# Three one-column tiles of a row norm put into one tile, and the weight tiles behind them 128 bytes lower

## The chip, the cores and the metric

The kernel runs on one core of a Trainium2 chip. A core has a matrix engine (TensorE, PE in the profile), a vector engine (VectorE, DVE), a scalar engine (ScalarE, ACT), GpSimd (POOL), a queue engine that issues most transfers here (SyncE, SP), and 16 DMA engines. Each engine runs its own instructions in order; they wait for each other by semaphores. SBUF is the on-chip memory of 128 partitions; a tile takes the same range of bytes in each partition. PSUM holds the results of matmuls. The metric is the time of one execution of the kernel on the device in microseconds (us), as the median of several runs. Lower is better.

## The reference

One layer of a bidirectional encoder on a sequence of 2048 rows of 1024 float32 values:

```
u      = rms_norm(x) * norm_mix_g
P      = u @ w_in                              # 1024 x 3600
v,x1,x2 = conv3(P[:, :1536])                   # hyena group, 512 channels each
z      = x1 * (h1 * v + d1 v);  z = x2 * (h2 * z + d2 z)     # long convolutions by FFT
q,k    = silu(conv3(P[:, 1536:2560]))          # mLSTM group, 4 heads, two directions
y      = concat(group_norm(z), group_norm(sigmoid(o) * mlstm(q, k, v, gates)))
h      = x + y @ w_out
h      = h + cross_attention(rms_norm(h), rms_norm(mem))     # mem: 256 rows
h      = h + square(relu(rms_norm(h) @ ff_w1)) @ ff_w2
out    = rms_norm(h)
```

rms_norm divides each row by the root of the mean of its squares plus 1e-6 and multiplies by a gain. The change touches the norm of x ahead of w_in and the norm of mem, both computed by the same function.

## The kernel before

**Products.** Every large product in float32 is made of three matmuls in a reduced-precision form: each operand is split into a high part (a cast, ScalarE) and a low part (operand minus the high part, VectorE); `mm3` adds high x high, high x low and low x high. In the profile these are lines L295, L296 and L297; the cast is L300 and the subtraction L301 in `split`. A matmul holds one operand of 128 columns still and streams the other past it, with up to 512 columns.

**Stages.** In the order of the program: the input projection (`sweep` for the columns that are convolved, with streamed blocks of 512 columns of `xh` and `xl`; `natural` for the others, with streamed weight blocks of 256 or 272 columns) is woven with first the filters' generation (`filters`) and then the long convolutions (`hyena`); then the mem projections (`memproj`) woven with the mLSTM; then the output projection and cross-attention (`attention`), then the MLP (`ffn`). By the trace, the first ends at about 1150 us, the mLSTM's weave with the mem projections at about 1400, attention at about 2090 and the MLP at the end.

**Input projection.** One pool of SBUF tiles, `i_sb` (`self.isb`), belongs to it and lives on through the mem projections. x is too large to be kept in split form, so `xh` and `xl` hold 1024 rows of it, transposed, and it is loaded and normalised three times by halves: first half, second half, first half again. With the two blocks of mem that gives 26 calls of `prep_norm` for 128 rows each. Each norm is followed by `prep_turn`: eight transposes on TensorE (L420), a cast (L300) and a subtraction (L301) for each half. `pop` lets one norm after the other go in between the matmul groups of `sweep` and `natural`. The weights come by `weights`: a load into `wn` (L327, from SP), a cast to `wh` (L300), a subtraction to `wl` (L301).

**A row norm.** `prep_norm` lets ScalarE sum the squares of the two halves of a row (L409), adds the sums on VectorE into the one-column tile `ms` (L411), scales and adds epsilon (L412), and calls `rsqrt`, which finds the inverse root on VectorE without a table: a shift and a subtraction on the bits (L150, L151) and three steps of three operations each (L153 to L155) on `y` and `t`, one-column tiles as well. Then `xn` is scaled in place by `y` and the gain (L414). The tiles `ms`, `y` and `t` have two buffers each, and each buffer of a tile of one column of 4 bytes takes 32 bytes of a partition.

**What sets the order.** The kernel is written as generators that `weave` lets run in turn by given weights. A scheduler takes the whole program, estimates times, and orders the instructions of each engine; an instruction that needs a buffer of a tile comes after the last use of the tile that had the buffer before. The order on every queue, SP's too, is fixed at that point. Addresses are given by the order in which a pool's tags are first used: after `ms` come the tags of `rsqrt`, and then `wh`, `wl`, `wn` and `sg`. `xh`, `xl`, `xn`, `st`, `P` and `cv` lie ahead of them.

**Other lines that the steps touch.** In `hyena`: L669 and L670 (loads of `dm` and `em`), L672, L675 and L676 (loads of `a`), L702 and L734 (matmuls in full float32, two passes), L703 and L736 to L740 (the complex product), L705 (store of `zg`), L766, L768 and L769 (norm of the result, its gain, its store `yh`). In the mem projections: `mt`, `kt` (split and transposed mem and keys). In attention: L1028 (load of w_out), L1100 (loads of the rows), L1106 (transposes of them), `act` (their split form).

Of the kernel before, what the change touches and what calls it, by code (L numbers as in the profile page):

```python
# [9 lines left out]
F32 = mybir.dt.float32  # L10
# [87 lines left out]
class Prog:  # L98
# [42 lines left out]
        else:  # L141
            self.nc.vector.tensor_copy(out, in_)

    def rsqrt(self, pool, ms, name):
        nc = self.nc
        shp = list(ms.shape)
        y = pool.tile(shp, F32, tag=name + "_y", name=name + "_y", bufs=2)
        t = pool.tile(shp, F32, tag=name + "_t", name=name + "_t", bufs=2)
        yi, mi = y.bitcast(I32), ms.bitcast(I32)
        nc.vector.tensor_scalar(yi, mi, 1, None, ALU.logical_shift_right)  # L150
        nc.vector.tensor_scalar(yi, yi, -1.0, float(0x5F3759DF), ALU.mult, ALU.add)  # L151
        for _ in range(3):
            nc.vector.tensor_tensor(t, y, y, ALU.mult)  # L153
            nc.vector.scalar_tensor_tensor(t, t, -0.5, ms, ALU.mult, ALU.mult)
            nc.vector.scalar_tensor_tensor(y, t, 1.5, y, ALU.add, ALU.mult)  # L155
        return y
# [247 lines left out]
    def prep_norm(self, xn, gain):  # L404
        nc, sb = self.nc, self.isb
        ss = sb.tile([128, 2], F32, tag="ss", name="ss", bufs=2)
        for h in range(2):
            junk = sb.tile([128, 512], F32, tag="st", name="junk", bufs=3)
            nc.scalar.activation(junk, xn[:, 512 * h:512 * h + 512], AF.Square, accum_out=ss[:, h:h + 1])  # L409
        ms = sb.tile([128, 1], F32, tag="ms", name="ms", bufs=2)  # L410
        nc.vector.tensor_tensor(ms, ss[:, 0:1], ss[:, 1:2], ALU.add)  # L411
        nc.vector.tensor_scalar(ms, ms, 1.0 / D, EPS, ALU.mult, ALU.add)  # L412
        rv = self.rsqrt(sb, ms, "xr")
        nc.vector.scalar_tensor_tensor(xn, xn, rv, gain, ALU.mult, ALU.mult)  # L414

    def prep_turn(self, xn, t):
# [1285 lines left out]
```

## Time and profile before

| | |
|---|---|
| median of 3 runs | 3382.24 us (3379.86 to 3386.33) |
| profiled execution | 3383.48 us |
| span of its trace | 3381.8 us |
| granted TensorE clock, mean | 0.979 |
| TensorE busy | 3194.3 us, 94% |
| weight loads | 2550.0 us, 75% |
| VectorE busy | 2042.5 us, 60% |
| ScalarE busy | 1492.4 us, 44% |
| GpSimd busy | 1269.8 us, 38% |
| HBM | 452.23 MB read, 219.18 MB written |

The span runs from the first to the last instruction of the trace; the time of the execution holds a little more on both sides. The page groups instructions by line, engine, operation and tiles (written as output<-inputs): busy time and the mean duration of one in ns, then the engine's idle time just before them, with what ended it. A matmul's duration there overlaps the next one's, so the rate is read from the distance of the starts. The timeline lists instructions by start (us from the span's start), duration, engine, line and tiles, with "xN" where N like instructions in a row are put together, and in brackets the idle time before them with what released them. The windows view gives each engine's busy time in stretches, the granted clock and the DMA engines' share.

### The profile page before, as it was taken

What the parts mean: (1) busy time and instruction counts of PE and PEld (TensorE: products, weight loads), DVE (VectorE), ACT (ScalarE), POOL (GpSimd) and SP (SyncE); (2) the same over time, 40 slices, a digit from 0 to 9 for tenths busy, and PEclk for the clock granted to TensorE, in tenths of its full rate; (3) what the DMA queues carried; (4) which work ended last, traced back from release to release, by engine and by line L of the source; (5) the groups of instructions that cost most, each with busy time, mean ns of one, the idle gap of its engine ahead of it and who ended that gap; (6) DMA issues with size and microseconds to landing.
All of it is one profiled execution on the core that took longest, in us unless ns stands there. A gap on an engine that the chain in (4) does not pass through costs nothing.

```text
span 3381.8 us, 46860 instructions
## 1 busy us (share of the span) xinstructions
PE 3194.3 (94%) x15671; PEld 2550.0 (75%) x15671; DVE 2042.5 (60%) x3711; ACT 1492.4 (44%) x2884; POOL 1269.8 (38%) x894
## 2 busy tenths in 40 slices
PE   6999999999898888799999999999999999999997
PEld 5646666677676788688887997788788887888876
DVE  7685225524546755777766554755855576555695
ACT  4344435523454235444444444555655543333335
POOL 2131001200222314544424012876766564434482
PEclk9999999999999999999999999999999999999998
DMA  5366889996998579857657444765654475444434
GB/s 165 117 208 206 286 282 256 271 325 238 241 240 279 172 229 273 275 154 231 184 162 253 147 132 161 224 205 179 207 167 158 147 244 171 128 140 135 133 94 159
DMA packets 480749, 674.55 MB, mean 199 GB/s; under 512 B 41738, under 2 KB 256848, under 8 KB 479484
## 3 DMA queue, kind: packets, MB, share of 16 engines
q1 hardware_dynamic: 478904, 668.70, 63.4%
q0 software_dynamic: 1600, 2.86, 0.4%
q8 instruction: 124, 2.03, 0.3%
q14 instruction: 117, 0.96, 0.1%
q10 hardware_dynamic: 4, 0.00, 0.0%
HBM read 452.23 MB, written 219.18 MB: 199 GB/s over the span
## 4 chain that ended last, share of the span: by engine, by line
PE 43%; DVE 7%; DMA 5%; issue 3%; POOL 2%; ACT 1%; SPq 1%; DVEq 0%; ACTq 0%; POOLq 0%
PE mm L295 9%; PE mm L297 9%; PE mm L296 9%; PE hy L297 5%; PE hy L295 4%; PE hy L296 4%; DVE wl L301 1%; DVE bl L1292 1%; POOL acc L1500 1%; DMA rw<-rows 1%; PE hy L1106 1%; DMA wr<-xs 1%; DMA wn<-in_x_dram 1%; DMA va<-vd 1%; DVE acc L1542 0%
## 5 line engine op out<-in xcount | busy, mean ns | idle before, releaser
L301 DVE TENSOR_TENSOR wl<-wn,wh 128x512 fp32r<-128x512 f32 (+1 forms) x352 | 274.6, 813 | 144.4 <-ACT wh L300 143.8
L1292 DVE TENSOR_TENSOR bl<-wr,bh 128x512 fp32r<-128x512 f32 x213 | 234.8, 1108 | 134.6 <-ACT bh L1291 132.2
L1291 ACT CAST ah<-w 128x512 fp32r<-128x512 f32 x284 | 176.2, 622 | 298.9 <-PE hy L296 152.7
L300 ACT CAST wh<-wn 128x512 fp32r<-128x512 f32 (+1 forms) x352 | 202.1, 617 | 216.2 <-PE mm L296 80.0
L295 PE MATMUL mm<-xh,wh 128*128 128x512 f32 x640 | 276.4, 432 | 8.7 <-ACT P L542 7.5
L739 POOL TENSOR_TENSOR b<-b,a 128x512 f32<-128x512 f32 x64 | 88.8, 1387 | 502.1 <-ACT b L737 201.1
L296 PE MATMUL mm<-xl,wh 128*128 128x512 f32 x640 | 266.4, 416 | 0.1
L297 PE MATMUL mm<-xh,wl 128*128 128x512 f32 x640 | 264.3, 413 | 0.3 <-DVE wl L301 0.3
L1292 DVE TENSOR_TENSOR al<-w,ah 128x512 fp32r<-128x512 f32 x236 | 226.9, 963 | 59.9 <-ACT ah L1291 59.7
L1291 ACT CAST bh<-wr 128x512 fp32r<-128x512 f32 x232 | 143.4, 621 | 244.3 <-PE mm L297 180.1
L297 PE MATMUL mm<-bh,al 128*128 128x512 f32 x576 | 224.4, 392 | 8.3 <-DVE al L1292 5.7
L295 PE MATMUL mm<-bh,ah 128*128 128x512 f32 x576 | 226.0, 392 | 0.0
L296 PE MATMUL mm<-bl,ah 128*128 128x512 f32 x576 | 225.0, 391 | 0.0
L295 PE MATMUL mm<-act,wh 128*128 128x512 f32 x512 | 201.4, 397 | 6.0 <-ACT wh L300 6.0
L296 PE MATMUL mm<-act,wh 128*128 128x512 f32 x512 | 203.0, 397 | 0.0
L297 PE MATMUL mm<-act,wl 128*128 128x512 f32 x512 | 201.1, 396 | 0.0
L1149 POOL TENSOR_TENSOR ssum<-ssum,sq 128x512 f32<-128x512 f32 x56 | 80.7, 1440 | 269.7 <-ACT sq L1148 268.2
L295 PE MATMUL hy<-bh,ah 128*128 128x512 f32 x448 | 175.2, 391 | 0.0
L296 PE MATMUL hy<-bl,ah 128*128 128x512 f32 x448 | 174.6, 390 | 0.0
L297 PE MATMUL hy<-bh,al 128*128 128x512 f32 x448 | 174.6, 390 | 0.0
L295 PEld LDWEIGHTS mm<-xh,wh 128*128 128x128 f32 x640 | 122.4, 191 | 56.7 <-issue 18.0
L295 PE MATMUL hy<-xh,ah 128*128 128x512 f32 x384 | 152.8, 398 | 7.6 <-ACT ah L1291 6.8
(379 smaller groups left out, 9021.1 us busy)
## 6 DMA issues: line engine op xcount, KB each, us to landing
wr<-hc SPq DMA_DIRECT2D x224, 256.0 KB
w<-in_ff_w_dram SPq DMA_DIRECT2D x176, 256.0 KB
a<-hd SPq DMA_DIRECT2D x128, 256.0 KB
hc<-t SPq DMA_DIRECT2D x128, 256.0 KB
wn<-in_w_in_dram SPq DMA_DIRECT2D x104, 256.0 KB
hc<-q SPq DMA_DIRECT2D x96, 256.0 KB
fs<-a SPq DMA_DIRECT2D x32, 512.0 KB
a<-fs SPq DMA_DIRECT2D x32, 512.0 KB
```

What stands on the lines that cost most here:

```text
L295: mm(ps, lh, rh, start=start, stop=False)
L296: mm(ps, lh, rl, start=False, stop=False)
L297: mm(ps, ll, rh, start=False, stop=stop)
L300: self.nc.scalar.copy(hi, src)
L301: self.nc.vector.tensor_tensor(lo, src, hi.bitcast(F32), ALU.subtract)
L739: nc.gpsimd.tensor_tensor(xt, xt, hi[:, m], ALU.mult)
L1106: nc.tensor.transpose(pt[:, 128 * k:128 * k + 128], yn[:, 128 * k:128 * k + 128], self.ident)
L1149: nc.gpsimd.tensor_tensor(ssum, ssum, sq, ALU.add)
L1291: self.nc.scalar.copy(hi, src)
L1292: eng.tensor_tensor(lo, src, hi.bitcast(F32), ALU.subtract)
L1500: nc.gpsimd.tensor_tensor(v, v, ms[2 * tp + n], ALU.mult)
```

## The change

`rsqrt` takes its two work tiles from the caller if there are any. `prep_norm` makes one tile `stat` of four columns under the tag `ms`, and hands its columns 0, 1 and 2 to the work: the sum, `y` and `t`. The other callers of `rsqrt` are as before.

```diff
-    def rsqrt(self, pool, ms, name):
+    def rsqrt(self, pool, ms, name, yt=None):
         nc = self.nc
         shp = list(ms.shape)
-        y = pool.tile(shp, F32, tag=name + "_y", name=name + "_y", bufs=2)
-        t = pool.tile(shp, F32, tag=name + "_t", name=name + "_t", bufs=2)
+        if yt is None:
+            y = pool.tile(shp, F32, tag=name + "_y", name=name + "_y", bufs=2)
+            t = pool.tile(shp, F32, tag=name + "_t", name=name + "_t", bufs=2)
+        else:
+            y, t = yt
...
-        ms = sb.tile([128, 1], F32, tag="ms", name="ms", bufs=2)
+        stat = sb.tile([128, 4], F32, tag="ms", name="ms", bufs=2)
+        ms = stat[:, 0:1]
         nc.vector.tensor_tensor(ms, ss[:, 0:1], ss[:, 1:2], ALU.add)
         nc.vector.tensor_scalar(ms, ms, 1.0 / D, EPS, ALU.mult, ALU.add)
-        rv = self.rsqrt(sb, ms, "xr")
+        rv = self.rsqrt(sb, ms, "xr", (stat[:, 1:2], stat[:, 2:3]))
         nc.vector.scalar_tensor_tensor(xn, xn, rv, gain, ALU.mult, ALU.mult)
```

The tags `xr_y` and `xr_t` (two buffers of 32 bytes each) are gone; a buffer of four columns still takes 32 bytes. So the two buffers of `wh`, those of `wl`, the three of `wn` and those of `sg` move down by 128 bytes; every other tile stays where it was. The number of instructions on each engine is the same. A buffer of `ms` is now in use until L414 of its norm, as `y` is in both versions.

## The prediction

> **What bounds the kernel now.** I began with the page: the span, the busy times and the costliest groups.
>
> ```profile
> span 3381.8 us, 46860 instructions
> PE 3194.3 (94%) x15671; PEld 2550.0 (75%) x15671; DVE 2042.5 (60%) x3711; ACT 1492.4 (44%) x2884; POOL 1269.8 (38%) x894
> L295 PE MATMUL mm<-xh,wh 128*128 128x512 f32 x640 | 276.4, 432 | 8.7 <-ACT P L542 7.5 <-ACT xh L300 1.2
> L296 PE MATMUL mm<-xl,wh 128*128 128x512 f32 x640 | 266.4, 416 | 0.1
> L297 PE MATMUL mm<-xh,wl 128*128 128x512 f32 x640 | 264.3, 413 | 0.3 <-DVE wl L301 0.3
> ```
>
> TensorE is busy for 94% of the span, and the three products of the input projection (1920 matmuls of 512 columns) are its largest groups. So the time is TensorE's work plus its holes. The windows view says where the holes are (columns: TensorE, weight load, DVE, ACT, POOL, granted clock, DMA share, GB/s).
>
> ```profile
> 100.00:600.00 500.00, 491.60 (x1852) 309.72 (x1851) 251.18 (x440) 216.69 (x377) 76.63 (x46) 1.00 0.72 232
> 600.00:700.00 100.00, 87.73 (x356) 63.30 (x355) 45.98 (x73) 50.56 (x83) 22.33 (x18) 0.90 1.02 271
> 800.00:900.00 100.00, 86.14 (x400) 60.05 (x399) 60.14 (x162) 45.06 (x97) 11.81 (x9) 0.91 0.87 260
> 900.00:1000.00 100.00, 100.00 (x414) 72.88 (x413) 49.33 (x76) 54.69 (x86) 19.30 (x14) 1.00 0.89 230
> 1000.00:1100.00 100.00, 90.94 (x370) 62.18 (x369) 59.75 (x101) 44.67 (x70) 27.99 (x17) 1.00 0.92 272
> ```
>
> From 100 to 600 us and from 900 to 1000 us TensorE hardly waits: a nanosecond per matmul saved or added there reaches the end. In the other three, part of it would go into waits. The clock below 1 stands in the windows with holes.
>
> Then I compared the spacing of matmuls of one shape, by the timeline's start times.
>
> ```profile
> 922.53 0.39 PE L296 MATMUL mm<-xl,wh 128*128 128x512 f32 x1
> ...
> 938.80 0.39 PE L297 MATMUL mm<-xh,wl 128*128 128x512 f32 x1
> ...
> 1360.93 0.39 PE L296 MATMUL mm<-wl,kt 128*128 128x512 f32 x1
> ...
> 1366.04 0.39 PE L297 MATMUL mm<-wh,kt 128*128 128x512 f32 x1
> ...
> 1754.17 0.40 PE L295 MATMUL mm<-act,wh 128*128 128x512 f32 x1
> ...
> 1756.25 0.39 PE L295 MATMUL mm<-act,wh 128*128 128x512 f32 x1
> ...
> 1768.49 0.39 PE L296 MATMUL mm<-act,wh 128*128 128x512 f32 x1
> ...
> 2179.74 0.39 PE L295 MATMUL mm<-xh,ah 128*128 128x512 f32 x1
> ...
> 2196.96 0.39 PE L296 MATMUL hy<-xl,ah 128*128 128x512 f32 x1
> ```
>
> - Input projection: 70 steps without a break take 16.27 us, 232.4 ns each. wh with kt: 22 steps in 5.11 us, 232.3.
> - Attention: after a break 9 steps take 2.08 us (231 ns each), and the next 54 take 12.24 us (226.7 each).
> - MLP: 76 steps take 17.22 us, 226.6 each.
>
> The input projection never settles at 227, over all its spacings the mean is 232.4 (1618 of them, the first at 32.3, the last at 1073.9 us). It is 231.6 to 233.0 in each 20 us slice at full clock, whatever the transfers do; here a slice with 232.3 and one with 232.1, at DMA shares of 0.15 and 1.06.
>
> ```profile
> 80.00:100.00 20.00, 20.00 (x92) 15.90 (x92) 14.01 (x24) 9.02 (x13) 0.00 (x0) 1.00 0.15 38
> 560.00:580.00 20.00, 19.73 (x73) 13.17 (x72) 7.88 (x13) 12.33 (x21) 6.40 (x5) 1.00 1.06 287
> ```
>
> So the extra 5.7 ns are not the transfers' doing. What does differ is where the operands lie. Bytes within a partition, modulo 256, as the two programs are placed: xh and xl 224, wh and wl 96 before and 224 after. In attention act and wh are both at 32, in the MLP bh, xh, ah and al all at 224. Each 512-column pairing with equal remainders runs at 227; those 128 apart (xh with wh, and wh at 96 with kt at 224, fifty us before attention's first) run at 232. Modulo 512 the pairing after the change will be 224 with 480: that is exactly the pairing of the MLP's xh with ah, in the last rows above.
>
> **The change, part by part.**
>
> *Operations.* None is added or removed on any engine. 26 norms still do the same 13 one-column operations, of 0.15 us where nothing is in the way:
>
> ```profile
> L153 DVE TENSOR_TENSOR xr_t<-xr_y x78: 146/159/1248, 6.5 to 1125.1; 128x1 f32<-128x1 f32 x78
> ```
>
>
> *Addresses.* xr_y and xr_t (128 bytes) go, and everything of that pool behind them moves down by 128: wh, wl, wn, sg.
>
> 512 columns: all 1920 at 226.8 instead of 232.4 would give 1920 x 5.6 ns = 10.8 us, one end; 0 is the other, if the place has no part in it. But the runs are short: matmuls of other lines and holes break them, 6.3 spacings in a row on the mean, and after a break 227 comes only after about nine steps. Putting attention's mean spacing at each place within a run (47 runs, the first from 1417.3, the last from 2053.6 us) on the input projection's runs gives 228.4: 1618 x 4.0 ns = 6.5 us; the MLP's means give 5.4 to 5.7. I take 6.5. Of it 1.35 us lie at 600 to 700, 840 to 900 and 1000 to 1100, where I let half go into longer waits: **-5.8**. The 96 matmuls of wh with kt add **-0.2**.
>
> 256 columns: here unequal remainders are the faster ones.
>
> ```profile
> 1151.89 0.28 PE L297 MATMUL mm<-wh,xl 128*128 128x256 f32 x1
> ...
> 1172.06 0.28 PE L296 MATMUL mm<-wl,xh 128*128 128x256 f32 x1
> ...
> 1675.08 0.28 PE L296 MATMUL mm<-wl,act 128*128 128x256 f32 x1
> ...
> 1693.80 0.28 PE L296 MATMUL mm<-wl,act 128*128 128x256 f32 x1
> ```
>
> 170 steps take 20.17 us (118.6 ns each) with remainders 128 apart, 156 steps take 18.72 us (120.0) with equal ones. 1152 such matmuls x 1.3 ns: **+1.4** (bounds 0 and +1.5).
>
> The Trainium skill, SBUF — State Buffer, "SBUF: two separate sides" says that on the engine side only the port pair of VectorE and GpSimd contends and that TensorE never waits on anyone; its "Operand start alignment" asks for no more than a multiple of the element size. By these the move is free and this part of the sum is 0 instead of -4.6. The 232.4 against 226.7 above speak against it, though no row has the same tiles at two places; it is the first rival.
>
> DVE, ACT and DMA: the slots of wn hold remainders 96 and 224 before and after; the subtractions that read them lie together (min/median/max in ns), and the long ones lie beside POOL's work: 0.
>
> ```profile
> L301 DVE TENSOR_TENSOR wl<-wn,wh x352: 671/686/1792, 22.1 to 2072.6; 128x512 fp32r<-128x512 f32 x172, 128x544 fp32r<-128x544 f32 x4
> ```
>
> *Order.* The scheduler places instructions by when a buffer is free. Before, only y waited for L414 of the norm two back; now the first operation, L411, does. That shifts the order in five stretches (0 to 80, 860 to 885, 960 to 1065, 1118 to 1160, 1400 to 1440 us; elsewhere nothing but a few casts at 1830).
>
> 0 to 80 us: L411 and L412 come behind another norm's L414 of 1.28 us, and some L414 come ahead of splits: one-column operations moved past each other, -0.5 to +1, taken as 0.
>
> 860 to 885 us: a pair of L702 and L734 is moved behind the transposes, and the last L414 no longer stands behind an L738 and an L740.
>
> ```profile
> 877.03 1.02 PE L702 MATMUL hy<-b,em 128*128 128x512 f32 x2
> 882.37 2.05 PE L702 MATMUL hy<-b,em 128*128 128x512 f32 x2 [2.59 <-ACT xh L300]
> 887.66 0.73 PE L295 MATMUL mm<-xh,wh 128*128 128x512 f32 x2 [1.01 <-ACT xh L300]
> 881.58 0.69 DVE L740 TENSOR_TENSOR b<-b 128x512 f32<-128x512 f32 x1
> 882.78 1.69 DVE L414 SCALAR_TENSOR_TENSOR xn<-xn,xr_y,g_mix 128x1024 f32<-128x1024 f32 x1
> ```
>
> Both waits (3.6 us) are for that norm's transposes and casts. The pair of 1.72 us fills the first: **-1.8**, bounds -3.6 and 0.
>
> 960 to 1065 us: pairs of L702 and L734 move by one to ten matmuls, and em, zg and dm change places on SP. Nearest are three waits of this stretch.
>
> ```profile
> 1016.10 1.10 PE L702 MATMUL hy<-b,em 128*128 128x512 f32 x2 [1.95 <-ACT P L542]
> 1023.46 1.10 PE L734 MATMUL hy<-a,dm 128*128 128x512 f32 x2 [1.53 <-DMA a<-zs]
> 1049.70 1.10 PE L702 MATMUL hy<-b,em 128*128 128x512 f32 x2 [2.41 <-DVE b L740]
> ```
>
> They can go (-5.9) or two more like them come (+4). Both ways have the same cause, so 0.
>
> 1118 to 1160 us: on SP the last store of yh, which waits for L768, now stands ahead of a load of w_in, and the attention loads behind it.
>
> ```profile
> 1147.49 0.38 SPq L327 DMA_DIRECT2D wn<-in_w_in_dram  x1
> 1150.32 0.32 SPq L769 DMA_DIRECT2D yh<-a  x1
> 1150.90 0.39 PE L296 MATMUL mm<-wl,xh 128*128 128x256 f32 x1 [0.71 <-DVE wl L301]
> ```
>
> If the store issues no earlier, the load goes out at 1150.64, 3.15 us late, and TensorE waits that much longer at 1150.9. But the DVE work before that store (two L766) also comes 1 to 2.5 us earlier: 0, bounds -0.7 and +3.2.
>
> 1400 to 1440 us: a w_out load behind rows loads, four transposes moved to the end of a run; TensorE's nearest wait is
>
> ```profile
> 1437.67 2.62 PE L1106 MATMUL hy<-ident,wn 128*128 128x128 f32 x12 [1.62 <-DMA wn<-in_x_dram]
> ```
>
> 0, within that wait either way.
>
> *Sum.* -5.8 - 0.2 + 1.4 - 1.8 = -6.4 on the profiled execution's 3383.48 us (span 3381.8 and 1.7 around it): 3377.1. That execution is 1.24 us above the median of three, 3382.24, so for the median I predict **3376 us**. All far ends at once would give -23 and +11.
>
> **The rivals.**
>
> 1. *The place has no part in it.* For: the 256-column spacing hardly moves (1%), and the settled groups all come after the unsettled ones. Against: wh with kt at 1360 us still has 232, attention 227 fifty us later, at like DMA shares. Then only -1.8 is left: 3380.4.
> 2. *The SP queue makes it slower.* The w_in load stays 3.15 us behind the yh store, the three xa_wk loads behind it too, and the hole at 1150.9 lets the clock fall as in the windows with holes (0.91 at 800 to 900: 9 us lost there, with four holes over 1 us some 2 to 3 each): +3.2 + 3, with the gain of the place as small as the MLP's means make it (5.4 - 0.5 - 1.4 = 3.5) and the holes at 960 to 1065 growing by 4: 3382.2 - 3.5 + 10.2 = 3389. It decides as soon as the store issues later than 1147.5. Against: L766 is earlier in the new order.
> 3. *It settles fully.* Equal remainders shorten the nine steps too: -10.8 + 1.4 - 1.8 = -11.2: 3371.
>
> **How the numbers follow.** Forecast 0.56 (its own range 3370 to 3381), first rival 0.17, second 0.16, third 0.11. A change of 0.2% (6.8 us) is about what a measurement here can tell from none. The forecast lies just at it: of its 0.56 I count 0.36 faster by more and 0.20 within. With the third: faster 0.47. Within: 0.20 and the first rival's 0.17, 0.37. Slower 0.16. Leaving out half of the second rival and the far ends of the third, the range is 3368 to 3388.
>
> **What would show it.** Right: spacing of mm<-xh,wh falls to 227 in the long runs (922 to 938 us before), mean duration of L296 and L297 there falls from 413 to 416 towards 409; the natural products' spacing goes from 118.6 to 120.0; the waits before 882.4 and 887.7 shrink; the span shortens steadily from 100 to 600 us by some 3 us. Wrong: spacing still 232 (first rival), a wait of 3 us at about 1150 for wl (second), or new waits of TensorE in the five stretches.

## The result and the profile after

The changed kernel took 3393.25 us (median of 7 runs, 3388.42 to 3399.68). Its ratio to the kernel before on the same chip is 1.0032, with an interval of 1.0018 to 1.0045: slower, by 6 to 15 us. The prediction was 3376 us, faster, and its range ended at 3388.

The page and the windows of the changed kernel, its profiled execution of 3399.68 us (lines are three higher than before from L148 on and four higher from L414 on: L298 to L300 are the three products, L303 and L304 the cast and the subtraction):

```profile
span 3397.9 us, 46862 instructions
PE 3195.0 (94%) x15671; PEld 2552.3 (75%) x15671; DVE 2050.2 (60%) x3711; ACT 1493.0 (44%) x2884; POOL 1270.1 (37%) x894
L298 PE MATMUL mm<-xh,wh 128*128 128x512 f32 x640 | 277.0, 434 | 8.7 <-ACT P L546 7.9
L299 PE MATMUL mm<-xl,wh 128*128 128x512 f32 x640 | 263.1, 412 | 0.0
L300 PE MATMUL mm<-xh,wl 128*128 128x512 f32 x640 | 264.0, 413 | 0.1
```

```profile
100.00:600.00 500.00, 489.02 (x1857) 310.07 (x1856) 251.55 (x442) 217.97 (x378) 75.07 (x45) 1.00 0.73 231
900.00:1000.00 100.00, 99.71 (x417) 73.28 (x416) 50.42 (x73) 54.60 (x86) 21.18 (x15) 1.00 0.85 224
1000.00:1100.00 100.00, 88.29 (x335) 59.05 (x334) 53.68 (x77) 44.34 (x69) 21.55 (x13) 0.95 0.92 254
1160.00:1180.00 20.00, 15.93 (x108) 15.38 (x107) 7.68 (x18) 4.87 (x10) 3.00 (x6) 0.83 0.64 178
```

TensorE's busy time is as before, and in the stretches without holes the matmuls do come closer: 1857 of them in 100 to 600 us (1852 before), 417 in 900 to 1000 (414). The loss lies in windows with holes. From 1000 to 1100 us there are 35 matmuls fewer than before (the same work comes some 10 us later here) and the granted clock is 0.95, not 1.00; from 1160 to 1180 the clock is 0.83.

The long run that had 232.4 ns per matmul, by the timeline of the changed kernel:

```profile
923.11 0.39 PE L299 MATMUL mm<-xl,wh 128*128 128x512 f32 x1
...
939.02 0.39 PE L300 MATMUL mm<-xh,wl 128*128 128x512 f32 x1
```

70 steps in 15.91 us are 227.3 ns each. So the place did what was forecast, and something else took more. The largest part of it is seen in the stretch that the prediction called 1118 to 1160 us, which comes 11 us later here. First before, then the changed kernel; the first and the last row of each are the same two matmuls, and the windows row tells before's clock from 1160 to 1180.

```profile
1146.92 0.28 PE L296 MATMUL mm<-mt,wh 128*128 128x256 f32 x1
...
1146.78 4.83 DVE L301 TENSOR_TENSOR wl<-wn,wh 128x512 fp32r<-128x512 f32 x4
...
1153.46 1.10 DVE L815 MEMSET pad<- 128x256 f32 x4 [1.86 <-DMA yh<-a]
...
1186.80 0.28 PE L297 MATMUL mm<-kt,wl 128*128 128x256 f32 x1
1160.00:1180.00 20.00, 16.84 (x145) 16.63 (x144) 4.72 (x12) 8.16 (x17) 0.00 (x0) 1.00 0.40 123
```

```profile
1157.83 0.29 PE L299 MATMUL mm<-mt,wh 128*128 128x256 f32 x1
...
1158.04 4.08 DVE L304 TENSOR_TENSOR wl<-wn,wh 128x512 fp32r<-128x512 f32 x3
1161.59 0.32 SPq L773 DMA_DIRECT2D yh<-a  x1
1162.01 0.39 SPq L330 DMA_DIRECT2D wn<-in_w_in_dram  x1
1164.82 1.09 DVE L819 MEMSET pad<- 128x256 f32 x4 [2.71 <-DMA yh<-a]
1165.74 0.62 ACT L303 CAST wh<-wn 128x512 fp32r<-128x512 f32 x1 [10.15 <-DMA wn<-in_w_in_dram]
1166.39 0.77 DVE L304 TENSOR_TENSOR wl<-wn,wh 128x512 fp32r<-128x512 f32 x1 [0.47 <-ACT wh L303]
1166.41 0.80 PE L298 MATMUL mm<-wh,xh 128*128 128x256 f32 x2 [3.02 <-ACT wh L303]
...
1203.72 0.28 PE L300 MATMUL mm<-kt,wl 128*128 128x256 f32 x1
```

Before, the last load of w_in issued 0.57 us after the first matmul shown (1147.49), ahead of the store of yh; four subtractions stood together on VectorE, and the pad memsets, which wait for that store's landing, stood behind all four. After, the load issues 4.18 us after that matmul, behind the store; three subtractions stand together, and the fourth stands behind the memsets. TensorE waits 3.02 us, and then the clock is lower. From the first to the last matmul it takes 45.9 us instead of 39.9.

### The profile page after: what moved, and what is told of

It is laid out like the page before. It is cut to its first block, busy times and chain, and to the rows that moved or that the text cites. A ratio compares the mean times of both kernels' runs of the same rounds, so it can differ in the third digit from the quotient of the medians.

```text
span 3397.9 us, 46862 instructions
## 1 busy us (share of the span) xinstructions
PE 3195.0 (94%) x15671; PEld 2552.3 (75%) x15671; DVE 2050.2 (60%) x3711; ACT 1493.0 (44%) x2884; POOL 1270.1 (37%) x894
## 4 chain that ended last, share of the span: by engine, by line
PE 54%; DMA 11%; DVE 8%; issue 2%; ACT 2%; POOL 1%; SPq 1%; DVEq 0%; ACTq 0%; POOLq 0%
PE mm L298 11%; PE mm L300 11%; PE mm L299 11%; PE hy L300 5%; PE hy L299 5%; PE hy L298 5%; DMA a<-hd 2%; DVE wl L304 2%; DMA va<-vd 1%; PE hy L757 1%; PE hy L724 1%; DMA wr<-xs 1%; PE hy L1110 1%; DMA wn<-in_w_in_dram 1%; DVE bl L1296 1%
## 5 line engine op out<-in xcount | busy, mean ns | idle before, releaser
L304 DVE TENSOR_TENSOR wl<-wn,wh 128x512 fp32r<-128x512 f32 (+1 forms) x352 | 276.1, 817 | 146.2 <-ACT wh L303 139.7
L303 ACT CAST wh<-wn 128x512 fp32r<-128x512 f32 (+1 forms) x352 | 202.3, 617 | 224.5 <-PE mm L299 78.9
L298 PE MATMUL mm<-xh,wh 128*128 128x512 f32 x640 | 277.0, 434 | 8.7 <-ACT P L546 7.9
L300 PE MATMUL mm<-xh,wl 128*128 128x512 f32 x640 | 264.0, 413 | 0.1
L299 PE MATMUL mm<-xl,wh 128*128 128x512 f32 x640 | 263.1, 412 | 0.0
L300 PE MATMUL mm<-bh,al 128*128 128x512 f32 x576 | 225.4, 394 | 5.8 <-DVE al L1296 3.2
L298 PE MATMUL mm<-bh,ah 128*128 128x512 f32 x576 | 227.1, 394 | 0.1
L299 PE MATMUL mm<-bl,ah 128*128 128x512 f32 x576 | 226.0, 392 | 0.0
L298 PE MATMUL mm<-act,wh 128*128 128x512 f32 x512 | 201.0, 396 | 6.7 <-ACT wh L303 6.7
L299 PE MATMUL mm<-act,wh 128*128 128x512 f32 x512 | 202.2, 396 | 0.0
L300 PE MATMUL mm<-act,wl 128*128 128x512 f32 x512 | 200.5, 395 | 0.0
L298 PE MATMUL hy<-bh,ah 128*128 128x512 f32 x448 | 175.2, 391 | 0.0
L299 PE MATMUL hy<-bl,ah 128*128 128x512 f32 x448 | 174.6, 390 | 0.0
L300 PE MATMUL hy<-bh,al 128*128 128x512 f32 x448 | 174.6, 390 | 0.0
L298 PEld LDWEIGHTS mm<-xh,wh 128*128 128x128 f32 x640 | 122.7, 192 | 56.2 <-issue 19.3
L298 PE MATMUL mm<-wh,xh 128*128 128x256 f32 (+1 forms) x512 | 155.3, 304 | 5.6 <-ACT wh L303 3.0
```

Of the source, the lines that this page charges most:

```text
L298: mm(ps, lh, rh, start=start, stop=False)
L299: mm(ps, lh, rl, start=False, stop=False)
L300: mm(ps, ll, rh, start=False, stop=stop)
L303: self.nc.scalar.copy(hi, src)
L304: self.nc.vector.tensor_tensor(lo, src, hi.bitcast(F32), ALU.subtract)
```

## The experiments

Throughout, "stretch" means the time between the same two matmuls in two traces, named by where they lie in the trace before; "spacing" is the mean distance of starts of the clean consecutive matmuls of the input projection, about 1615 of 512 columns and 1060 of 256 columns in each trace. "Remainder" is wh's place in its partition modulo 256 bytes (96 before, 224 after; xh and xl at 224).

**The place alone.** A wider `ms` moves wh, wl, wn and sg up by 128 bytes. Every engine's order stays that of before.

```diff
-        ms = sb.tile([128, 1], F32, tag="ms", name="ms", bufs=2)
+        ms = sb.tile([128, 24], F32, tag="ms", name="ms", bufs=2)[:, 0:1]
```

> The kernel before, with the one-column tile ms made 24 columns wide (96 bytes) and only its first column used: wh, wl, wn and sg lie 128 bytes higher, so that wh and wl have remainder 224 modulo 256 as in the changed kernel; every engine's order is that of the kernel before. Theory A (the place gains, the order loses): spacing of mm<-xh,wh falls from 232.4 to about 228.5 and that of mm<-wh,xh rises to 120; time 4 to 6 us below before, ratio 0.9985 (0.9975 to 0.9995). Theory B (the faster matmuls are what loses: they meet the transfers at other times): the same spacings, but new waits between 985 and 1070 us and 6 to 11 us slower, ratio 1.002 to 1.003.

3376.57 us, ratio 0.9984 (0.9972 to 0.9997).

```profile
919.79 0.39 PE L296 MATMUL mm<-xl,wh 128*128 128x512 f32 x1
...
935.70 0.39 PE L297 MATMUL mm<-xh,wl 128*128 128x512 f32 x1
```

The same 70 steps take 15.91 us, as in the changed kernel. The move alone gives the closer spacing and makes the kernel faster.

**The order alone.** The changed kernel with its tile widened, so that every tile stands where it stood before.

```diff
-        stat = sb.tile([128, 4], F32, tag="ms", name="ms", bufs=2)
+        stat = sb.tile([128, 24], F32, tag="ms", name="ms", bufs=2)
```

> The changed kernel with the shared tile made 24 columns wide: every address is that of the kernel before, the order on every engine that of the changed kernel. Theory A: spacing 232.4 as before, and the whole loss without the gain: 14 to 18 us above before, ratio 1.0045 (1.003 to 1.006), with new waits at about 1050 and 1150 us. Theory B: same as before within 3 us, ratio 0.999 to 1.001.

3389.87 us, ratio 1.0023 (1.0010 to 1.0036), 3 to 12 us slower; spacing 232.4, as before. The order alone makes it slower, but by less than the 14 to 18 us that were expected. In its trace the stretch 1146 to 1186 takes 43.7 us, where the changed kernel has 45.9 and before 39.9: TensorE's hole is as long (2.91 us), and less of the clock is lost behind it.

**The changed kernel again**, without an edit, for the trace to trace scatter.

> The changed kernel again, on the same chip as the others of this call. Both theories: ratio 1.002 to 1.0045, some 11 us.

3388.7 us, ratio 1.0026 (1.0010 to 1.0041). With the first seven runs: 1.0027, give or take 0.0009 (two standard errors, 19 runs).

**The last store of yh off SP's queue.** The changed kernel, with that one store issued by GpSimd, so that the load of w_in no longer stands behind it.

```diff
-                nc.sync.dma_start(out=yh[:, js], in_=sq)
+                (nc.gpsimd if j2 == 7 else nc.sync).dma_start(out=yh[:, js], in_=sq)
```

> The changed kernel with the last store of yh issued from GpSimd, whose L768 it waits for, in place of SyncE; otherwise the same order. The load of w_in that stood behind it on SP goes out some 3.5 us earlier. If that store is what made 3.0 us of TensorE's waiting and 3 us at half clock at about 1150 us: 4 to 6 us below the changed kernel, ratio to before about 1.0015, and no wait of 3 us there. If the load would have been late anyhow: as the changed kernel, ratio 1.003.

3388.47 us, ratio 1.0026 (1.0014 to 1.0038): nothing gained. The timeline says why.

```profile
1150.40 0.40 SPq L330 DMA_DIRECT2D wn<-in_w_in_dram  x1
...
1152.82 0.60 POOL L773 DMA_DIRECT2D yh<-a  x1 [0.30 <-POOL a L772]
...
1157.19 1.09 DVE L819 MEMSET pad<- 128x256 f32 x4 [4.11 <-issue]
...
1158.22 0.68 DVE L304 TENSOR_TENSOR wl<-wn,wh 128x512 fp32r<-128x512 f32 x1
...
1158.95 0.39 PE L299 MATMUL mm<-wl,xh 128*128 128x256 f32 x1 [3.65 <-DVE wl L304]
```

The load now issues 2.4 us ahead of the store. But VectorE idles 4.11 us in front of the memsets, which start 0.4 us after that store has landed (4.0 us after its issue); the fourth subtraction comes right behind them, and TensorE waits 3.65 us for it, for wl instead of wh. The wait only moved: the stretch 1146 to 1186 is 48.6 us (45.9 and 48.4 in the two traces of the changed kernel, 40.0 before). In the two traces above 48 us a second hole near the stretch's end, where transposes wait for a load of xa_wq, is a part of it: 3.8 us, with the clock low behind it, against 3.16 before.

**The pad memsets off VectorE too.** The kernel of the last experiment, with the four pad memsets on GpSimd.

```diff
-                    nc.vector.memset(t, v)
+                    nc.gpsimd.memset(t, v)
```

> The changed kernel with the last store of yh issued from GpSimd and the four memsets of pad put on GpSimd as well, so that neither SP's load of w_in nor VectorE's last subtraction for it stands behind that store. If these two places in the order cost what stands at 1146 to 1186 us (45.9 and 48.4 us in the two traces of the changed kernel, 40.0 and 41.1 with the order of before): that stretch falls to about 41 us and the time by 5 us, ratio to before 1.001 (1.000 to 1.002). If the wait only moves again: ratio 1.0025.

3384.22 us, ratio 1.0019 (1.0001 to 1.0036); the stretch is 43.8 us, not the 41 expected.

```profile
1149.62 0.06 DVE L849 MEMSET mm<- 1x4 f32 x1 [4.28 <-issue]
...
1149.72 0.69 DVE L304 TENSOR_TENSOR wl<-wn,wh 128x512 fp32r<-128x512 f32 x1
...
1150.47 0.39 PE L299 MATMUL mm<-wl,xh 128*128 128x256 f32 x1 [2.91 <-DVE wl L304]
```

Now VectorE idles 4.28 us at the next memsets, two of 0.06 us on a tile of the same pool, and the subtraction still stands behind them. TensorE's wait is 2.91 us, as in the order experiment, whose stretch was as long without any of these edits: that 43.8 is less than 48.6 does not show a gain by the pads.

**All of it off VectorE.** As before, with those two memsets on GpSimd as well.

```diff
-            nc.vector.memset(mm[:, 0, 0, 0], 0.0)
-            nc.vector.memset(mm[:, 0, 1, 15], 0.0)
+            nc.gpsimd.memset(mm[:, 0, 0, 0], 0.0)
+            nc.gpsimd.memset(mm[:, 0, 1, 15], 0.0)
```

> The run pads_yh with the two small memsets of mm on GpSimd as well, which there still held VectorE's last subtraction until the store of yh had landed. Theory: the wait of TensorE of 2.9 us at 1150 goes, the stretch that is 1146 to 1186 us in the kernel before falls from 43.8 to about 41 us, and the time to 4 to 7 us below the changed kernel, ratio 1.0005 to 1.0015.

```profile
1153.99 0.29 PE L299 MATMUL mm<-mt,wh 128*128 128x256 f32 x1
...
1154.10 0.40 SPq L330 DMA_DIRECT2D wn<-in_w_in_dram  x1
...
1157.74 0.69 DVE L304 TENSOR_TENSOR wl<-wn,wh 128x512 fp32r<-128x512 f32 x1 [0.95 <-ACT wh L303]
...
1194.34 0.28 PE L300 MATMUL mm<-kt,wl 128*128 128x256 f32 x1
```

The stretch is 40.3 us, what it was before, and the hole of 3 us for that load's weights is gone. So its loss is explained, by one trace: a load on SP stood behind the issue of one store, and a subtraction on VectorE behind memsets that wait for the landing of the same store; to free SP alone gives nothing (VectorE alone was not tried). The whole kernel took 3385.58 us, ratio 1.0017 (1.0004 to 1.0031). All runs of this kernel and of the one of the last experiment together stand at +6.0 us against before (give or take 2.7), where the changed kernel has +9.1 (give or take 2.9). The difference has the right sign, but is no larger than its uncertainty, and smaller than the 4 to 7 us expected of this kernel: the cure is shown by the stretch, not by the total.

**Sharing in the later norms only.** The first eight norms take their three tiles as before, the other 18 share one; the tile is widened so that the places are those of the place experiment.

```diff
+        stat = sb.tile([128, 24], F32, tag="ms", name="ms", bufs=2)
+        ms, self.normed = stat[:, 0:1], self.normed + 1
...
+        rv = self.rsqrt(sb, ms, "xr", (stat[:, 1:2], stat[:, 2:3]) if self.normed > 8 else None)
```

> The tile shared in 18 of the 26 norms, all but the first eight; y and t of the first eight stay tiles of their own, and the shared tile is 24 columns wide, so that wh and wl have remainder 224. The order on every engine comes out as in the kernel before. Theory A (the sharing itself costs nothing; what loses is the order that it gives the first eight norms and all that the scheduler then moves later): as the run place, ratio 0.9985 (0.997 to 0.9995). Rival (the wait of L411 for L414 costs in each norm, or a shared tile is slower): 18/26 of the loss stays, ratio 1.002.

3374.7 us, ratio 0.9982 (0.9966 to 0.9998). The program's order is that of before on every engine. So 18 of 26 norms share a tile, each first operation waits for a longer-lived buffer, and no loss is seen: the sharing itself costs nothing that these runs show, and the whole reordering, as far as 1440 us, comes from the first eight norms. That it spreads by the times that the scheduler estimates from there on is likely, but the scheduler was not followed.

**More buffers for the shared tile.** Five instead of two (16 columns, for the same place as in the place experiment), which gives a third order.

```diff
-        stat = sb.tile([128, 4], F32, tag="ms", name="ms", bufs=2)
+        stat = sb.tile([128, 16], F32, tag="ms", name="ms", bufs=5)
```

> The changed kernel with five buffers of 16 columns for the shared tile in place of two of four: wh and wl have remainder 224, L411 need not wait for the L414 of the norm two back, and the scheduler finds a third order, different from both on every engine. If the wait for the buffer is what gave the bad order: ratio 0.9985 to 1.000. If any order that differs from that of before is apt to lose some us in the stretches that the transfers bound: ratio 1.001 to 1.004.

3384.9 us, ratio 1.0008 (0.9990 to 1.0026); the stretch 1146 to 1186 is 45.8 us. The loss at that place came with this order too; the total lies between the two others and is not told apart from before.

**Sharing in norms 1 and 2 only, and in norms 3 and 4 only**, with the places of the place experiment. The first differs in order from before at 15 to 100 us alone, the second at 20 to 61, 1414 to 1442 and 1831 to 1843 us.

```diff
+        rv = self.rsqrt(sb, ms, "xr", (stat[:, 1:2], stat[:, 2:3]) if self.normed <= 2 else None)
...
+        rv = self.rsqrt(sb, ms, "xr", (stat[:, 1:2], stat[:, 2:3]) if 3 <= self.normed <= 4 else None)
```

> The tile shared in the first two norms alone, the shared tile 24 columns wide (remainder 224). The order differs from that of before only between 15 and 100 us, on PE by a few filter matmuls. If the start's order by itself costs the 3 us that the traces of the changed kernel show at 0 to 100 us: 0.9990 to 0.9998, that is 3 us above place. If the loss needs the later stretches: as place, 0.9988.

> The tile shared in the third and fourth norm alone (remainder 224). The order differs between 20 and 61 us and at 1414 to 1442 and 1831 to 1843 us, in the last two as in the changed kernel; at 860 to 1186 us it is that of before. If the loss of the changed kernel lies at 944 to 1186 us: as place or at most 2 us above, 0.9985 to 0.9996. If it lies in the start and at 1400 us: 1.001 or more.

3377.2 us, ratio 0.9994 (0.9981 to 1.0007), and 3375.27 us, ratio 0.9988 (0.9975 to 1.0001). Both lie with the place experiment: parts of the start's order cost too little to be seen in the total.

**The place, taken further.** The place experiment with other widths of `ms`: 40 columns move wh by 256 bytes (the remainder stays 96), 16 by 64 (remainder 160), 32 by 192 (remainder 32). The order is always that of before.

```diff
-        ms = sb.tile([128, 1], F32, tag="ms", name="ms", bufs=2)
+        ms = sb.tile([128, 40], F32, tag="ms", name="ms", bufs=2)[:, 0:1]
```

> The kernel before with ms 40 columns wide: wh and wl lie 256 bytes higher, remainder 96 as before, order as before. If the remainder modulo 256 decides: spacing of mm<-xh,wh 232.4 and time as before, ratio 1.000 (0.999 to 1.001). If any move would do (another bank, distance to xh): spacing 228 and ratio 0.9985.

> The run place again, for a closer interval, beside place256 on the same chip. If the remainder's gain of 3 us at 100 to 560 us reaches the end and nothing else counts: 2 to 5 us below place256_b. If what it gains is waited off later, or place256's own 3 us below before are real: the two within 2 us.

> The run place256 again: order and remainder of the kernel before, everything behind ms 256 bytes higher. Same as before, ratio 0.9995 to 1.0005, unless a move by 256 bytes does something that the spacing does not show (then 0.9985 again).

> The kernel before with ms 16 columns wide: wh and wl 64 bytes higher, remainder 160 beside the 224 of xh and xl; a look for the spacing. If 512-column matmuls settle only at equal remainders: about 232 for mm<-xh,wh, and 118 to 119 for mm<-wh,xh. If only a distance of 128 is slow: 228 and 120.

> The run place64 with rounds (order of before, remainder 160 beside 224). Its one look had spacings of 229.6 for mm<-xh,wh and 117.0 for mm<-wh,xh, both below the kernel before (232.4 and 118.9): by 1618 and 1152 of them 4.5 and 2.2 us less on TensorE, against 6.2 less and 1.4 more for place. If that reaches the end: ratio 0.998 (0.997 to 0.999), 2 us below place.

> The kernel before with ms 32 columns wide: wh and wl 192 bytes higher, remainder 32 beside 224, 64 from it on the other side (order of before). If only the distance counts: the spacings and the time of place64. If the sign counts: spacings of their own.

| remainder of wh | kernels | 512 columns, ns | 256 columns, ns | ratio to before |
|---|---|---|---|---|
| 96 | before | 232.4 | 118.9 | 1 |
| 96 | moved by 256, twice | 232.4 | 118.9 | 0.9987 (0.9972 to 1.0001), 1.0006 (0.9995 to 1.0018) |
| 224 | moved by 128, twice | 228.6 | 119.7 | 0.9984 (0.9972 to 0.9997), 0.9995 (0.9982 to 1.0008) |
| 160 | moved by 64 | 229.9 | 115.5 to 115.9 | 0.9989 (0.9978 to 1.0000); a single run 3369.91 us |
| 32 | moved by 192 | 233.3 | 116.8 | 0.9999 (0.9981 to 1.0016) |

The medians are 3376.68 and 3382.19 us for 256, 3375.51 for the second run of 128, 3377.47 for 64, 3380.64 for 192. The median durations of one group (the second of the three numbers, in ns) differ in the same sense: after the move by 64 first, by 192 second.

```profile
L296 PE MATMUL mm<-xl,wh x640: 387/392/798, 32.6 to 1064.6; 128*128 128x512 f32 x160
```

```profile
L296 PE MATMUL mm<-xl,wh x640: 388/395/801, 32.4 to 1074.3; 128*128 128x512 f32 x160
```

A run of 57 steps with remainder 160:

```profile
914.76 0.39 PE L297 MATMUL mm<-xh,wl 128*128 128x512 f32 x1
...
927.81 0.39 PE L297 MATMUL mm<-xh,wl 128*128 128x512 f32 x1
```

13.05 us, 228.9 ns each: neither 227 nor 232, and neither of the two outcomes that were expected for the move by 64. All traces with one remainder agree within about 0.2 ns at 512 columns, whatever their order; a move by 256 leaves the spacing as it was. So the spacing hangs on the place modulo 256, and "equal remainders" is not the whole rule. x itself was never moved; that the pair counts, and not the weights' place alone, rests on attention, where the weights lie at 32 as well and settle at 226.7 with an operand at 32. Runs of one program scatter by 4 to 7 us (standard deviation), so a gain of 4 us needs many. Taken together, the place experiment, its second run and the kernel with 18 shared norms stand at 0.9988 (give or take 0.0006, 36 runs), 4.1 us faster; the two moves by 256 at 0.9999 (give or take 0.0007, 24 runs).

The version moved by 128 bytes in before's order beats both kernels. The one moved by 64 and the one with 18 shared norms are as good, and are not told apart from it.

## Why the prediction was wrong

The two parts of the change, told apart: the place gives -4.1 us (0.9988, give or take 2.0 us), the changed kernel is at +9.1 (1.0027, give or take 2.9), so by difference the order costs about 13 us, give or take 3.5. The order experiment alone has about 8 (3 to 12). The two figures only just agree: the loss by the order is shown, its size lies at some 8 to 13 us. In the new order the totals do not show the place's gain: the changed kernel's second set of runs lies 0.6 us above the order experiment's on the mean, give or take 5.6. The prediction had -4.6 for the place and -1.8 for the order.

*512 and 256 columns.* Right. Predicted were spacings of 228.4 and 120.0, measured 228.6 and 119.7; -4.6 predicted, -4.1 measured in the order of before (1152 times 1.3 ns is 1.5 us, not the 1.4 of the sum; the difference is too small to matter). The stretch 100 to 560 us shortens by 2.4 us on the mean of the traces, where "some 3" were to be seen. The first rival, that the place has no part in it, falls; so does the third, full settling. The durations, a sign that the prediction named, were a weak one: L299 fell from 416 to 412, L300 stayed at 413. By the Trainium skill, SBUF — State Buffer, "SBUF: two separate sides", TensorE waits on no one at its side of SBUF, and the prediction read the move as free from that; the section says nothing of where a matmul's two operands lie to each other. The rows of the place experiment disagree with that reading (228.6 against 232.4 ns), and the measurement decides.

*0 to 80 us, taken as 0 with a far end of +1.* Mis-sized. The stretch 0 to 100 takes 102.9 us on the mean of five traces in the order after, and 100.3 in the order before: +2.6. Two waits at the start, from the second trace of the changed kernel, were not there before:

```profile
55.71 0.63 PE L424 MATMUL mm<-ident,xn 128*128 128x128 f32 x4 [1.31 <-DVE xn L418]
...
58.59 1.13 PE L211 MATMUL hy<-b,w 66*128 66x512 f32 x2 [0.86 <-DMA b<-in_c_feat_dram]
```

The one-column operations were costed by their own length and not by what they delay: the transposes wait for xn.

*860 to 885 us, -1.8.* Not borne out, though a number near it can be read: 862 to 944 us takes 79.8 instead of 82.0 us on the mean of five traces each, -2.2. But four matmuls of the pairs of L702 and L734 have left this stretch and stand behind 944 us now. The windows of the stretches 862 to 903 and 944 to 984 show it, first in the place experiment (the weights' place of the changed kernel, the order of before), then in the changed kernel:

```profile
859.90:900.50 40.60, 35.48 (x131) 23.81 (x132) 26.21 (x61) 20.99 (x40) 9.30 (x7) 0.92 0.91 257
941.90:980.40 38.50, 38.50 (x157) 28.09 (x156) 17.86 (x28) 20.74 (x33) 8.15 (x6) 1.00 0.99 270
```

```profile
864.90:903.80 38.90, 34.41 (x127) 22.56 (x128) 25.78 (x59) 19.09 (x37) 7.52 (x6) 0.91 0.84 228
945.20:986.00 40.80, 40.51 (x161) 28.78 (x160) 19.48 (x29) 22.59 (x35) 10.45 (x7) 1.00 0.97 259
```

There are 131 matmuls and then 127 in the one, 157 and then 161 in the other, which takes 1.9 us more on the mean with next to no wait in it. From 862 to 984 us together, where the work is the same, the difference is -0.3 us: the work was moved, and the waits were not filled. The waits for xh, 2.59 and 1.01 before, are 0.24 after; but two others came, of the transposes that were now ahead of the moved pair:

```profile
880.37 1.06 PE L424 MATMUL mm<-ident,xn 128*128 128x128 f32 x8 [2.03 <-DVE xn L418]
...
886.57 1.06 PE L424 MATMUL mm<-ident,xn 128*128 128x128 f32 x8 [1.72 <-DVE xn L418]
887.88 0.90 PE L298 MATMUL mm<-xh,wh 128*128 128x512 f32 x2 [0.24 <-ACT xh L303]
```

*960 to 1065 us, 0 with ends of -5.9 and +4.* Within the ends, on the bad side: 984 to 1070 us +2.5 on the mean. In the changed kernel's first trace:

```profile
1020.70 1.10 PE L706 MATMUL hy<-b,em 128*128 128x512 f32 x2 [3.30 <-ACT P L546]
...
1029.82 1.10 PE L738 MATMUL hy<-a,dm 128*128 128x512 f32 x2 [1.68 <-DMA a<-zs]
...
1046.46 0.38 SPq L330 DMA_DIRECT2D wn<-in_w_in_dram  x1
...
1057.06 0.64 ACT L303 CAST wh<-wn 128x544 fp32r<-128x544 f32 x1 [8.58 <-DMA wn<-in_w_in_dram]
...
1058.46 0.68 DVE L744 TENSOR_TENSOR b<-b 128x512 f32<-128x512 f32 x1
...
1059.30 2.05 PE L706 MATMUL hy<-b,em 128*128 128x512 f32 x2 [5.91 <-DVE b L744]
```

The same three waits were 1.95, 1.53 and 2.41 us before. The largest stands behind a late load: w_in, issued at 1046.46, is cast at 1057.06, 10.6 us later (1039.77 and 1047.46 before: 7.7), and VectorE does the product for TensorE only behind that weight's subtraction. But this stretch is unsteady: 85.5 to 96.1 us in the order after and 81.6 to 91.4 in the order before, over all the traces. How much of the 2.5 is the order stays open.

*1118 to 1160 us, 0 with a far end of +3.2.* This is the step that failed. Measured: +7.4 (47.6 us on the mean of three traces, against 40.2 on the mean of five), and +3.7 in the order experiment's trace. It failed at two points. The store was taken to issue earlier, since two L766 move up; counted from the first matmul shown, it issues after 3.76 us, and after 3.40 before; the load, now behind it, goes out after 4.18 us instead of 0.57. And the far end held the wait alone, while the clock that is lost behind it is as much: 0.83 over 20 us from 1160 to 1180, that is 3.4 us, beside the 3.02 of the wait. At a third point it was incomplete: of the queues in which something waits for that store, only SP's was followed, and not VectorE's, where a subtraction had fallen behind memsets that wait for the same store. In the changed kernel this costs nothing more, but it keeps the wait when SP's queue is freed. The second rival had the wait and the clock (3.2 and 3) and the condition (a store later than 1147.5), and came to 3389; it was given 0.16 because of the L766. Its mechanism was the right one, though incomplete, and its hole came elsewhere: the wait for wl that it names (0.71 us at 1150.90 before) is 0.72 after, and the new one comes 4 us behind it, for wh of the late load.

*1400 to 1440 us, 0.* Right: 1350 to 1450 us does not differ.

The measured terms of the order, +2.6, -0.3, +2.5 and +7.4, with about -1.2 from all the rest, sum to some 11 us, between the 8 and the 13 of the totals. The prediction put four stretches at zero, most of them because ends lay on both sides. One of them held most of the answer, and the rows of its load and its store had been quoted; the memset's wait for yh on VectorE, which had not, lies in the trace before, 1.86 us long, where it delayed no one.

## What to carry to other kernels

A change to tiles changes two things, the addresses behind them and the order that a scheduler finds, and each can be made alone: a wider tile moves the addresses and leaves the order, a padded new tile does the reverse. Where an instruction that waits for a slow event (here a store's landing, 3 to 4 us) changes places, look on every queue for what newly stands behind that event, memsets into reused memory too, and price the wait with the clock that it costs. A list of moved stretches with ends of both signs should not be summed as zero when TensorE is busy for 94% of the time: there is hardly a wait to lose, and many to gain. And where a stretch gets shorter, count its matmuls before calling it a gain: work may have been moved out of it.

## What the runs showed of the hardware

- At the places tried, the spacing of matmuls hangs on where the two operands lie to each other modulo 256 bytes: 228.6, 229.9, 232.4 and 233.3 ns at 512 columns with the weights at remainders 224, 160, 96 and 32 (x at 224), and 119.7, about 115.7, 118.9 and 116.8 ns at 256 columns, where weights and x change roles. The best place for one shape is not that for the other. Why is not shown by any row.
- A hole of 3.02 us at TensorE was followed by a granted clock of 0.83 over 20 us, so it cost about double its length. The price is not fixed: within these 20 us the clock stands at 0.50 for 6.8 us (3.4 us lost); behind the hole of 2.91 us in the order experiment it does so for 3.4 us (1.7 lost), and behind the hole of 3.16 us at 1177 us before it stays at 1.00. After the pad and mm memsets had gone to GpSimd, the stretch was 40.3 us again.
- A memset of 0.06 us held VectorE for 4.28 us, and ran just behind the landing of a store that took 4.2 us to land; with the memset on GpSimd TensorE's wait of 2.91 us was gone. Its duration says nothing of its price.
